# Latent and dilated attention in one pipeline, with norm factors moved into transposes and exponents

## The chip, the cores and the metric

The kernel runs on one core of a Trainium2 chip. A core has TensorE (PE, matrix products and transposes into PSUM), VectorE (DVE), ScalarE (ACT) and GpSimd (Pool), which work from queues of their own and wait for one another by semaphores, and DMA queues, most of them issued by SyncE (SP). The metric is the device time of one execution in microseconds, as the median over several executions. Lower is better.

## The reference, cut to what matters

The program computes two transformer blocks on 256 tokens of 1024 channels. The first block has an even layer, an odd layer and an MLP behind each. The change touches the mixers of these two layers:

```
def even_mixer(h, ...):            # 256 x 1024
    u = h @ w_in                   # 1024 x 2976
    c_q, c_kv, k_r, u_dil = ...    # 384, 256, 32 and 2304 columns
    q = rms_norm(c_q, q_lat_norm) @ w_uq        # 8 heads x (64 + 32)
    kv = rms_norm(c_kv, kv_lat_norm) @ w_ukv    # 8 heads x (64 + 64)
    k = concatenate([k_nope, broadcast(k_r)])   # one k_r for all heads
    q, k = rms_norm(q, mla_qn), rms_norm(k, mla_kn)
    q, k = rope on the last 32 of 96 columns of each
    o_a = dense_causal_attention(q, k, v_a)     # scale 96 ** -0.5
    qd = apply_rope(rms_norm(qkv[:, :, 0], dil_qn), positions)
    kd = apply_rope(rms_norm(qkv[:, :, 1], dil_kn), positions)
    o_b = dilated_mixture(qd, kd, v_d)          # 3 groups x 4 heads of 64
    return concatenate([o_a, o_b]) @ w_out      # 768 x 1024
```

The dilated mixture is a softmax over the keys of three groups together. The odd mixer has 4 differential heads (two softmaxes each) and 8 block heads, all with 64 channels and, at 256 tokens, plain causal masks.

## The kernel before

Tokens lie in two tiles of 128 partitions. A product with weights is made of three products of halves (`mm3`, lines 346 to 348): a weight block arrives by DMA (`raw`), ACT rounds it (`whi`, line 268), DVE subtracts (`wlo`, line 270), and PE multiplies. Weight blocks stand in one sequence through the program; between them stand the *items* of the modulation: half of a 1 MB block of `in_ada_w`, which DVE multiplies and sums in one instruction (lines 308 and 324). They are needed much later, and `spread` sets them among the weight blocks. Of the even stage's 24 items the last 16 are held back to stand ahead of the out projection (`late`), and `tick(n)` takes up n of them.

A recording layer notes every operation of a stage and then sets an order for each engine by priorities and dependences; each engine runs its own queue strictly in that order. So the order can be listed, but not an engine's times.

The even stage (`even`, from line 972) runs: projections 0 to 2 of `w_in` (`dil(i)` for the later ones), whose columns go to `ulat` (latents and `k_r`) and `ud` (dilated q, k and v); the norms of the latents, their transposes (`lh`, `ll`), the products with `w_uq` and `w_ukv`; `normrope` for q and k. `normrope` squares on ACT, sums on DVE (line 685), takes the reciprocal root on DVE in small steps (lines 385 to 390), multiplies by table A, which holds the norm weights and the cosine (691), adds the part that Pool rotated with table B (688, 692), and multiplies by the reciprocal root (693). The tables are made on Pool (lines 666 to 673) from the cosine and sine that ACT computes. Projections 3 and 4 follow, and then a pipeline over four pairs of latent heads with five steps: transposes of q and k (`m_qk`), scores (`m_s`, line 351 through `causal_scores`), maxima, exponents and scaling by the inverse sum (`m_e`), transposes of P (`m_t`), products with v (`m_o`). `pipe` runs step s of job j at turn j + s. Projection 5 and the dilated `normrope` (`dprep`) stand between its first turns. A second pipeline of the same form over four dilated heads follows it (`d_qk` to `d_o`), and behind it the out projection (`out_mm`) and the residual.

A causal mask is added in PSUM by a product with the identity (`masks`, bf16, 128 rows), ahead of the product of q and k (float32, which takes two PE instructions a block). Score tiles come from a pool of two, small PSUM tiles `pt` and `pg` from pools of two each. `cp` puts three of four copies on ACT and the fourth on DVE.

## Time and profile before

| | us |
|---|---|
| median of 3 runs (2333.54 to 2338.28) | 2334.09 |
| the profiled execution | 2334.84 |
| its span, first to last instruction | 2333.0 |
| PE busy in the span | 2210.0 (95%) |
| DVE busy | 1922.9 (82%) |
| ACT busy | 1378.4 (59%) |
| Pool busy | 201.6 (9%) |
| mean granted clock of PE | 0.971 |

The rows that the text rests on are in a section of their own below. In a timeline a row begins with its start and its duration in microseconds, both counted from the start of the span; rows of the same kind in sequence are joined (x4). The duration of one instruction reaches beyond the start of the next where they overlap. The even stage ends near 246 us, the odd stage runs from about 440 to 600.

### The profile page before, as it was taken

The page shows a single profiled execution, that of the slowest core. Times are in us where ns is not written, and L with a number is a line of the kernel's source. Part 1 is how long each engine was busy: PE and PEld are TensorE (multiplying, and loading weights), DVE is VectorE, ACT ScalarE, POOL GpSimd, SP SyncE. Part 2 cuts the span into 40 slices and gives each one's busy share as a digit, 9 for nine tenths or more (in the row PEclk, how much of TensorE's full clock was granted, in tenths as well). Part 3 has the DMA queues.
Part 4 walks back from the last instruction along what each step waited for, and adds up shares of the span by engine and source line. Part 5 has one row for each costly group of instructions (what it writes and reads, how often), then busy time and mean ns, then how long its engine had stood idle before and what let it go on. Part 6 is the DMA issues. An engine that isn't in the chain of part 4 may idle for free. (4 is left out here: it accounts for less than half of the span.)

```text
span 2333.0 us, 30681 instructions
## 1 busy us (share of the span) xinstructions
PE 2210.0 (95%) x11405; PEld 1821.6 (78%) x11405; DVE 1922.9 (82%) x2616; ACT 1378.4 (59%) x1884; POOL 201.6 (9%) x276
## 2 busy tenths in 40 slices
PE   4979999999999997999999999999999999999997
PEld 3766888777788896579997788888878878788875
DVE  6984889687798667669866799999888899898996
ACT  4532644555645534444444678787777776777764
POOL 1320001311200121110000100000000000000010
PEclk9986999999999999999999999999999999999998
DMA  8641798661679398249936799999989989898981
GB/s 330 227 166 64 267 349 320 206 237 51 228 290 355 144 307 235 67 179 376 373 140 261 281 358 371 338 378 340 361 320 368 356 337 365 327 363 339 363 313 55
DMA packets 102333, 647.44 MB, mean 278 GB/s; under 512 B 12037, under 2 KB 19685, under 8 KB 28064
## 3 DMA queue, kind: packets, MB, share of 16 engines
q1 hardware_dynamic: 88512, 618.83, 70.0%
q0 software_dynamic: 12976, 25.41, 4.4%
q8 instruction: 91, 1.49, 0.2%
q10 hardware_dynamic: 688, 1.16, 0.2%
q14 instruction: 66, 0.54, 0.1%
HBM read 637.21 MB, written 8.15 MB: 277 GB/s over the span
## 5 line engine op out<-in xcount | busy, mean ns | idle before, releaser
L270 DVE TENSOR_TENSOR wlo<-raw,whi 128x1024 fp32r<-128x1024 f32 (+1 forms) x551 | 662.5, 1228 | 125.8 <-ACT whi L268 117.8
L268 ACT CAST whi<-raw 128x1024 fp32r<-128x1024 f32 (+1 forms) x551 | 561.8, 1049 | 339.8 <-PE pg L347 94.3
L270 DVE TENSOR_TENSOR wlo<-rawm,whi 128x1024 fp32r<-128x1024 f32 x422 | 505.9, 1238 | 37.0 <-ACT whi L268 25.4
L268 ACT CAST whi<-rawm 128x1024 fp32r<-128x1024 f32 x422 | 426.3, 1052 | 82.7 <-PE sc L348 30.6
L346 PE MATMUL pg<-th,whi 128*128 128x256 f32 x1024 | 293.8, 291 | 2.5 <-ACT th L527 1.8
L347 PE MATMUL pg<-tl,whi 128*128 128x256 f32 x1024 | 293.3, 287 | 0.6 <-DVE tl L522 0.6
L348 PE MATMUL pg<-th,wlo 128*128 128x256 f32 x1024 | 292.9, 287 | 0.4 <-DVE wlo L270 0.4
L346 PEld LDWEIGHTS pg<-th,whi 128*128 128x128 f32 x1024 | 198.3, 195 | 9.7 <-issue 3.3
L347 PEld LDWEIGHTS pg<-tl,whi 128*128 128x128 f32 x1024 | 200.2, 196 | 4.9 <-issue 2.0
L348 PEld LDWEIGHTS pg<-th,wlo 128*128 128x128 f32 x1024 | 200.1, 195 | 1.4 <-DVE wlo L270 1.2
L347 PE MATMUL sc<-wlo,xo 128*128 128x512 f32 x448 | 179.2, 400 | 8.4 <-DVE wlo L270 8.4
L347 PE MATMUL sc<-wlo,th 128*128 128x512 f32 x448 | 177.0, 395 | 2.8 <-DVE wlo L270 2.8
L348 PE MATMUL pg<-whi,gg 128*128 128x512 f32 x448 | 175.9, 393 | 3.5 <-PEq L2095 3.5
L347 PE MATMUL pg<-wlo,gg 128*128 128x512 f32 x448 | 178.8, 399 | 0.0
L346 PE MATMUL sc<-whi,xo 128*128 128x512 f32 x448 | 176.8, 395 | 0.0
L346 PE MATMUL sc<-whi,th 128*128 128x512 f32 x448 | 176.4, 394 | 0.0
L348 PE MATMUL sc<-whi,xo 128*128 128x512 f32 x448 | 175.8, 392 | 0.0
L348 PE MATMUL sc<-whi,th 128*128 128x512 f32 x448 | 175.0, 391 | 0.7 <-POOL th L1991 0.7
L346 PE MATMUL pg<-whi,gg 128*128 128x512 f32 x448 | 161.1, 392 | 1.4 <-ACT gg L369 1.4
L347 PE MATMUL po<-wlo,ah 128*128 128x512 f32 x344 | 134.3, 391 | 1.1 <-DVE wlo L270 1.1
L346 PE MATMUL po<-whi,ah 128*128 128x512 f32 x344 | 135.2, 393 | 0.0
L348 PE MATMUL po<-whi,al 128*128 128x512 f32 x344 | 133.9, 389 | 0.0
(549 smaller groups left out, 3938.1 us busy)
## 6 DMA issues: line engine op xcount, KB each, us to landing
rawm<-in_moe_w SPq DMA_DIRECT2D x196, 1024.0 KB, 6.4
raw<-in_moe_w SPq DMA_DIRECT2D x140, 1024.0 KB, 6.4
raw<-in_mlp_w SPq DMA_DIRECT2D x64, 1024.0 KB, 7.0
raw<-in_ada_w SPq DMA_DIRECT2D x48, 1024.0 KB, 8.4
raw<-in_w_ada SPq DMA_DIRECT2D x35, 1024.0 KB, 6.8
raw<-in_ffn_w SPq DMA_DIRECT2D x20, 1024.0 KB, 8.0
rawm<-in_w_ada SPq DMA_DIRECT2D x13, 1024.0 KB, 6.6
rawm<-in_ffn_w SPq DMA_DIRECT2D x13, 1024.0 KB, 8.2
```

The source lines that it names most:

```text
L268: self.order(self.nc.scalar.copy(h, src))
L270: self.order((self.nc.gpsimd if pool else self.nc.vector).tensor_sub(l, src, h.bitcast(F32)))
L346: mm(out, a[0], b[0], start=start, stop=False, skip_group_check=True)
L347: mm(out, a[0], b[1], start=False, stop=False, skip_group_check=True)
L348: return mm(out, a[1], b[0], start=False, stop=stop, skip_group_check=True)
```

## The change

In the even stage:

- `k_r` is rotated once, for all heads (`kr`), with the rotated part from Pool (`kt`). The sum of squares of k is that of its 64 own columns (`ksq`, squared on ACT) plus that of `k_r` (`kss`).
- The weights of the norms on the first 64 columns of q and k become one column factor `gc`, with which ACT scales k's transposes as it copies them out of PSUM. Table A is applied to q's last 32 columns only.
- q's reciprocal root is no longer multiplied into q; it goes into the maxima and into the scale of the exponent (`qr`, `factors`). One chain of small steps gives the roots of q and k together.
- Copies of v, of ud and of q's and k's transposes are on ACT.
- One pipeline runs over eight jobs, first the four latent pairs, then the four dilated heads, with projection 5 and `dprep` between its turns and the out projection of the latent heads at turns 9 and 10. Value products of some jobs are written into the free quarter of a score tile (`put`). 24 items are held back in place of 16, and six turns take up four each.

In both stages `causal_scores` treats the two heads of a job block by block, both masks first, and the value products of two heads alternate.

```diff
+    def turned(self, src, nh, d, rd, tabs, rt):
+        Bt, n, o = tabs[1], rd // 2, d - rd
+        for h in range(2):
+            b = Bt[:, :, None, h * n:(h + 1) * n].to_broadcast([128, 2, nh, n])
+            self.nc.gpsimd.tensor_tensor(rt[:, :, :, h * n:(h + 1) * n], src[:, :, :, o + (1 - h) * n:o + (2 - h) * n],
+                                         b, ALU.mult)
...
-        for u, (q, k) in enumerate(units):
-            r = ps[:, u]
-            self.mm(r[:, 0:128], self.eyeb, self.cmask(0), True, False)
-            self.mm(r[:, 0:128], q[:, 0:128], k[:, 0:128], False, True)
-            self.mm(r[:, 128:256], q[:, 128:256], k[:, 0:128], True, True)
-            self.mm(r[:, 256:384], self.eyeb, self.cmask(0), True, False)
-            self.mm(r[:, 256:384], q[:, 128:256], k[:, 128:256], False, True)
+        for c, a, b in ((0, 0, 0), (128, 1, 0), (256, 1, 1)):
+            if a == b:
+                for u in range(2):
+                    self.mm(ps[:, u, c:c + 128], self.eyeb, self.cmask(0), True, False)
+            for u, (q, k) in enumerate(units):
+                self.mm(ps[:, u, c:c + 128], q[:, a * 128:a * 128 + 128], k[:, b * 128:b * 128 + 128], a != b, True)
...
-        nc.vector.tensor_scalar(mx, mx, -scale, None, op0=ALU.mult)
+        if factors:
+            m = mx.rearrange("p (a b) -> p a b", a=2)
+            nc.vector.tensor_tensor(m, m, factors[1], ALU.mult)
+            sc = [[factors[0][:, t, u:u + 1] for t in range(2)] for u in range(2)]
+        else:
+            nc.vector.tensor_scalar(mx, mx, -scale, None, op0=ALU.mult)
+            sc = 2 * [2 * [scale]]
...
-            nc.scalar.activation(P[:, u, 0:128], ps[:, u, 0:128], AF.Exp, bias=mx[:, u:u + 1], scale=scale,
+            nc.scalar.activation(P[:, u, 0:128], ps[:, u, 0:128], AF.Exp, bias=mx[:, u:u + 1], scale=sc[u][0],
                                  accum_out=sm[:, u:u + 1])
-            nc.scalar.activation(P[:, u, 128:384], ps[:, u, 128:384], AF.Exp, bias=mx[:, 2 + u:3 + u], scale=scale,
...
-                        n.cp(ud[:, t, c0 + k - 672:c0 + w - 672], ps[:, k:])
+                        nc.scalar.copy(ud[:, t, c0 + k - 672:c0 + w - 672], ps[:, k:])
...
+            kr = lat.tile([128, 2, 32], F32, name="kr")
+            kt = lat.tile([128, 2, 32], F32, name="kt")
+            kss = lat.tile([128, 2, 1], F32, name="kss")
+            own = ulat[:, :, 640:672]
+            nc.scalar.activation(kt, own, AF.Square)
+            nc.vector.reduce_sum(kss, kt, axis=AX.X)
+            n.turned(own[:, :, None], 1, 32, 32, (None, tk[1]), kt[:, :, None])
+            nc.vector.tensor_tensor(kr, own, tk[0][:, :, 64:], ALU.mult)
+            nc.vector.tensor_tensor(kr, kr, kt, ALU.add)
+            gc = ph.tile([96, 2], F32, name="gc")
+            nc.gpsimd.memset(gc, 1.0)
+            for i, nm in enumerate(("mla_q_norm", "mla_k_norm")):
+                nc.gpsimd.dma_start(gc[0:64, i:i + 1], dram(n.I[nm], 0, [[1, 64], [1, 1]]))
+            nc.gpsimd.tensor_tensor(gc[:, 0:1], gc[:, 0:1], gc[:, 1:2], ALU.mult)
...
+                nc.scalar.activation(ksq[:, t], pv[:, :, :64], AF.Square)
                 nc.scalar.copy(k[:, t, :, :64], pv[:, :, :64])
-                nc.vector.tensor_copy(v[:, t], pv[:, :, 64:])
-                nc.gpsimd.tensor_copy(k[:, t, :, 64:], ulat[:, t, None, 640:672].to_broadcast([128, 8, 32]))
+                nc.gpsimd.tensor_copy(k[:, t, :, 64:], kr[:, t, None].to_broadcast([128, 8, 32]))
+                nc.scalar.copy(v[:, t], pv[:, :, 64:])
-            for src, tab, w in ((q4, tq, tmp), (k, tk, ulat)):
-                n.normrope(src, 8, 96, 32, tab, w[:, :, :768].rearrange("p t (h c) -> p t h c", c=96),
-                           w[:, :, 768:].rearrange("p t (h c) -> p t h c", c=32))
+            ss = ph.tile([128, 2, 16], F32, name="qss")
+            sq = tmp[:, :, :768].rearrange("p t (h c) -> p t h c", c=96)
+            rt = tmp[:, :, 768:].rearrange("p t (h c) -> p t h c", c=32)
+            nc.scalar.activation(sq, q4, AF.Square)
+            nc.vector.reduce_sum(ss[:, :, 0:8], sq, axis=AX.X)
+            n.turned(q4, 8, 96, 32, tq, rt)
+            nc.vector.reduce_sum(ss[:, :, 8:], ksq, axis=AX.X)
+            nc.vector.tensor_tensor(ss[:, :, 8:], ss[:, :, 8:], kss.to_broadcast([128, 2, 8]), ALU.add)
+            n.rstd(ss, ss, 96)
+            nc.vector.tensor_tensor(k, k, ss[:, :, 8:, None].to_broadcast([128, 2, 8, 96]), ALU.mult)
+            nc.vector.tensor_tensor(q4[:, :, :, 64:], q4[:, :, :, 64:], tq[0][:, :, None, 64:].to_broadcast([128, 2, 8, 32]), ALU.mult)
+            nc.vector.tensor_tensor(q4[:, :, :, 64:], q4[:, :, :, 64:], rt, ALU.add)
+            ph.tile([128, 56], F32, name="even_out")
+            qr = ph.tile([128, 2, 2, 8], F32, name="qr")
+            for i, f in enumerate((96 ** -0.5, -96 ** -0.5)):
+                nc.vector.tensor_scalar(qr[:, i], ss[:, :, 0:8], f, None, op0=ALU.mult)
...
+                d = att.tile([128, 6, T], F32, name="qk", bufs=2)
+                for i, src in enumerate((q4, k)):
...
+                    nc.scalar.activation(d[:96, 2 * i:2 * i + 2], p[:96], AF.Copy, scale=gc[:, 0:1] if i else 1.0)
+                return d[:, 0:2], d[:, 2:4]
...
-                return n.causal_exp(st, 96 ** -0.5, att)[0]
+                return n.causal_exp(st, None, att, factors=[qr[:, i, :, 2 * j:2 * j + 2] for i in range(2)])[0]
...
+            def put(j):
+                return room[j + 3][:, 3] if j + 3 in room else n.ps.tile([128, 512], F32, name="pg", tag="g")[:, :T]
...
-            next(main)
-            dprep(qd, tdq)
-            dil(5)
-            oT += [n.big.tile([128, KB, T], F32R, name=nm, tag=nm) for nm in ("th", "tl")]
-            next(main)
-            next(main)
-            dprep(kd, tdk)
-            for _ in main:
-                n.tick(2)
+                po = put(j)
+                for i in range(2):
+                    for u in range(2):
+                        n.mm(po[64 * u:64 * u + 64, 128 * i:T], v[:, i, 2 * j + u], st[u][:, T * i:T + 128 * i], i == 0, i == 1)
+                if not oM:
+                    oM.append(n.big.tile([128, 2, 4, T], F32R, name="oM", tag="xn"))
+                n.split(oM[0][:, 0, j], oM[0][:, 1, j], po)
...
+                d = att.tile([128, 6, T], F32, name="qk", bufs=2)
+                for i in range(3):
+                    p = n.ps.tile([128, 2, T], F32, name="pt", tag="t")
+                    for a in range(2):
+                        src, g = ((qd, kd)[(2 * i + a) // 3], (2 * i + a) % 3)
                         for t in range(2):
-                            n.tp(p[:, 0, t * 128:(t + 1) * 128],
+                            n.tp(p[:, a, t * 128:(t + 1) * 128],
+                    n.cp(d[:, 2 * i:2 * i + 2], p)
+                dT[j // 2] = d[:, 0:3], d[:, 3:6]
+                return dT[j // 2]
...
+                p1 = room[4 + j] = n.pa.tile([128, 4, T], F32, name="sc", tag="acc")
...
+                n.order(nc.vector.reduce_max(mx[:, 0:1], p0[:, :384], axis=AX.X))
...
+                r = put(4 + j)[b:b + 64]
                 for g in range(3):
-                    n.mm(r[:, :T], vd[:, 0, g * 4 + j], st[g][:, 0:T], g == 0, False)
+                    n.mm(r, vd[:, 0, g * 4 + j], st[g][:, 0:T], g == 0, False)
                     n.mm(r[:, 128:T], vd[:, 1, g * 4 + j], st[g][:, T:384], False, g == 2)
-                if u:
...
-            for _ in n.pipe(4, [d_qk, d_s, d_e, d_t, d_o]):
-                n.tick(2)
-            acc = n.out_acc()
-            n.out_mm(acc, ("eout", 0), oT, range(0, 4), 0, True, False)
-            n.out_mm(acc, ("eout", 1), oT, range(4, 6), 0, False, True, (0, 2))
+            def both(m, d):
+                return lambda j, st: m(j, st) if j < 4 else d(j - 4, st)
+            acc = []
+            for i, _ in enumerate(n.pipe(8, [both(*f) for f in ((m_qk, d_qk), (m_s, d_s), (m_e, d_e), (m_t, d_t), (m_o, d_o))])):
+                if i == 0:
+                    dprep(qd, tdq)
+                elif i == 1:
+                    dprep(kd, tdk)
+                elif i == 3:
+                    dil(5)
+                    oT += [n.big.tile([128, KB, T], F32R, name=nm, tag=nm) for nm in ("th", "tl")]
+                elif i == 9:
+                    acc = n.out_acc()
+                    n.out_mm(acc, ("eout", 0), (oM[0][:, 0], oM[0][:, 1]), range(0, 2), 0, True, False)
+                elif i == 10:
+                    n.out_mm(acc, ("eout", 0), (oM[0][:, 0], oM[0][:, 1]), range(2, 4), 2, False, False)
+                if 3 <= i < 9:
+                    n.tick(4)
+            n.out_mm(acc, ("eout", 1), oT, range(0, 2), 0, False, True, (0, 2))
...
-                for m in range(2):
-                    h = 2 * (j - 4) + m
-                    r = po[64 * m:64 * m + 64]
-                    n.mm(r[:, :T], vm[:, 0, h], st[m][:, 0:T], True, False)
-                    n.mm(r[:, 128:T], vm[:, 1, h], st[m][:, T:384], False, True)
+                for i in range(2):
+                    for m in range(2):
+                        n.mm(po[64 * m:64 * m + 64, 128 * i:T], vm[:, i, 2 * (j - 4) + m], st[m][:, T * i:T + 128 * i], i == 0, i == 1)
...
-        (b1.even, lambda: b1.even_items(), side(0), 16, ("eout", 0)),
+        (b1.even, lambda: b1.even_items(), side(0), 24, ("eout", 0)),
```

Three places show the new order. DVE, while the latents are normalised; `lss` is the sum of squares of the latents, `tmp` their scaled copy. Before:

```order
L385 TENSOR_SCALAR rsa<-lss 128x2
L1016 TENSOR_SCALAR tmp<-ulat,lss 128x384
L386 TENSOR_SCALAR lss<-rsa 128x2
L1016 TENSOR_SCALAR tmp<-ulat,lss 128x384
L388 TENSOR_TENSOR rsu<-lss 128x2
```

and now:

```order
L1052 TENSOR_TENSOR kr<-ulat,tkA 128x64
L270 TENSOR_TENSOR wlo<-raw,whi 128x768
L385 TENSOR_SCALAR rsa<-lss 128x2
L1050 TENSOR_REDUCE kss<-kt 128x2
L386 TENSOR_SCALAR lss<-rsa 128x2
L388 TENSOR_TENSOR rsu<-lss 128x2
L1053 TENSOR_TENSOR kr<-kr,kt 128x64
L389 SCALAR_TENSOR_TENSOR rsu<-rsu,rsa 128x2
```

The two operations on `kr`, the second of which reads Pool's `kt`, now stand inside the reciprocal root of the kv latents.

PE, behind the fifth projection (512 columns) and around the last (416 columns), before, where the last projection ends:

```order
L347 MATMUL pg<-wlo,th 128x416
L348 MATMUL pg<-whi,tl 128x416
L355 MATMUL pt<-eye,k 96x128 x4
L355 MATMUL pt<-eye,q 96x128 x4
L355 MATMUL pt<-eye,k 96x128 x4
L351 MATMUL sc<-kT,qT 128x128 x2
```

and now, where the fifth ends:

```order
L347 MATMUL pg<-wlo,th 128x512
L348 MATMUL pg<-whi,tl 128x512
L355 MATMUL pt<-eye,q 96x128 x3
L355 MATMUL pt<-eye,k 96x128 x4
L351 LDWEIGHTS eyeb
L351 MATMUL sc<-masks,eyeb 128x128
```

The transposes of k moved ahead of all but one product of the last projection.

PE, among the dilated scores, before:

```order
L351 LDWEIGHTS eyeb
L351 MATMUL pg<-masks,eyeb 128x128
L351 MATMUL pg<-kT,qT 128x128
L351 LDWEIGHTS eyeb
L351 MATMUL sc<-masks,eyeb 128x128
L351 MATMUL sc<-kT,qT 128x128
```

and now, where they begin:

```order
L355 MATMUL pt<-eye,P 128x128 x6
L351 MATMUL pg<-PT,v 64x256 x2
L351 MATMUL pg<-PT,v 64x128 x2
L351 LDWEIGHTS eyeb
L351 MATMUL pg<-masks,eyeb 128x128
L351 MATMUL pg<-qk 128x128
```

The dilated scores now follow a latent pair's transposes of P and value products, and the next pair's follow them.

## Rows read from the trace of the kernel before

**Rows 1.** Busy time by stretch: stretch, length, each engine, granted clock (PEclk), DMA.

```profile
83.50:115.24 31.74, 29.73 (x130) 23.22 (x129) 31.74 (x45) 18.81 (x21) 2.72 (x2) 1.00 0.63 221
115.24:135.96 20.72, 15.88 (x82) 14.72 (x81) 19.18 (x23) 4.04 (x7) 8.78 (x4) 0.84 0.56 201
135.96:170.00 34.04, 25.03 (x148) 19.45 (x147) 31.86 (x83) 18.02 (x54) 4.04 (x8) 0.85 0.35 115
170.00:212.00 42.00, 40.61 (x137) 26.33 (x136) 15.14 (x33) 12.06 (x27) 0.00 (x0) 0.51 0.23 84
212.00:240.60 28.60, 27.15 (x130) 19.65 (x129) 17.06 (x22) 7.79 (x14) 2.27 (x2) 1.00 0.43 166
260.00:280.00 20.00, 20.00 (x151) 19.24 (x151) 19.69 (x21) 13.79 (x19) 0.00 (x0) 1.00 0.99 378
520.00:560.00 40.00, 40.00 (x235) 31.05 (x234) 30.74 (x80) 22.10 (x74) 2.55 (x2) 1.00 0.20 69
```

**Rows 2.** Timeline of DVE: start, us, engine, line, operation, [idle before <-releaser].

```profile
94.77 1.28 DVE L1049 COPY v<-py 128x512 f32<-128x512 f32 x2
...
99.69 1.75 DVE L691 TENSOR_TENSOR k<-k,tkA 128x1536 f32<-128x1536 f32 x1
...
104.57 1.28 DVE L324 SCALAR_TENSOR_TENSOR acc<-raw,cs,acc 128x1024 f32<-128x1024 f32 x1
...
105.85 1.22 DVE L270 TENSOR_TENSOR wlo<-raw,whi 128x1024 fp32r<-128x1024 f32 x1
...
127.25 1.75 DVE L693 TENSOR_TENSOR k<-k,hss 128x1536 f32<-128x1536 f32 x1
...
135.96 0.42 DVE L716 TENSOR_REDUCE mx<-sc 128x2 f32<-128x256 f32 x1 [1.45 <-PE sc L351]
```

**Rows 3.** Timeline of PE around the last projection.

```profile
115.24 0.60 PE L355 MATMUL pt<-eye,q 128*96 128x128 f32 x4
115.59 0.44 PE L346 MATMUL pg<-whi,th 128*128 128x416 f32 x1
...
129.06 1.06 PE L355 MATMUL pt<-eye,k 128*96 128x128 f32 x4 [4.17 <-DVE k L693]
```

**Rows 4.** Timeline of PE, dilated scores.

```profile
172.17 0.29 PE L351 MATMUL pg<-masks,eyeb 128*128 128x128 bf16 x1
...
173.11 0.29 PE L351 MATMUL sc<-masks,eyeb 128*128 128x128 bf16 x1
```

**Rows 5.** Timeline of PE: scores in the even stage, then in the odd stage.

```profile
144.38 0.22 PE L351 MATMUL sc<-masks,eyeb 128*128 128x128 bf16 x1 [3.30 <-ACT P L724]
144.43 0.66 PE L351 MATMUL sc<-kT,qT 96*128 96x128 f32 x4
...
546.39 0.71 PE L351 MATMUL sc<-kT,qT 64*128 64x128 f32 x4
547.03 0.23 PE L351 MATMUL sc<-masks,eyeb 128*128 128x128 bf16 x1
547.19 0.48 PE L351 MATMUL sc<-kT,qT 64*128 64x128 f32 x2
547.61 0.23 PE L351 MATMUL sc<-masks,eyeb 128*128 128x128 bf16 x1
```

**Rows 6.** Timelines of Pool (the rope tables) and DVE (the kv latents).

```profile
65.72 0.96 POOL L669 TENSOR_TENSOR tqA<-gq,cos 128x16 f32<-128x16 f32 x1 [0.43 <-ACT cos L409]
...
79.49 0.29 POOL L673 TENSOR_SCALAR tdkB<-tdkB 128x32 f32<-128x32 f32 x1
...
72.59 0.71 DVE L1017 TENSOR_SCALAR tmp<-ulat,lss 128x256 f32<-128x256 f32 x2
```

**Rows 7.** Timeline of PE behind the out projection.

```profile
240.58 0.60 PE L355 MATMUL pt<-eye,x 128*128 128x128 f32 x4
```

**Rows 8.** Groups by line from 100 to 241 us, ACT: count | busy, mean ns | idle.

```profile
L361 ACT COPY qT<-pt 96x512 f32<-96x512 f32 x4 | 2.3, 582 | 9.0 <-PE pt L355 9.0
...
L722 ACT ACTIVATE P<-sc,mx 128x128 f32<-128x128 f32 x8 | 2.9, 368 | 1.1 <-DVE mx L718 1.1
```

More of the change, by code (lines that the diff above doesn't have):

```diff
@@ L721, in causal_exp @@
         for u in range(2):
-            nc.scalar.activation(P[:, u, 0:128], ps[:, u, 0:128], AF.Exp, bias=mx[:, u:u + 1], scale=scale,
+            nc.scalar.activation(P[:, u, 0:128], ps[:, u, 0:128], AF.Exp, bias=mx[:, u:u + 1], scale=sc[u][0],
                                  accum_out=sm[:, u:u + 1])
-            nc.scalar.activation(P[:, u, 128:384], ps[:, u, 128:384], AF.Exp, bias=mx[:, 2 + u:3 + u], scale=scale,
+            nc.scalar.activation(P[:, u, 128:384], ps[:, u, 128:384], AF.Exp, bias=mx[:, 2 + u:3 + u], scale=sc[u][1],
                                  accum_out=sm[:, 2 + u:3 + u])
@@ L759, in start @@
         self.sm = e(self.tc.tile_pool(name="sm", bufs=4, reuse_waits="tile"))
-        self.sm.tile([128, 48], F32, name="even_out", bufs=1)
+        self.sm.tile([128, 16], F32, name="even_out", bufs=1)
         self.big = e(self.tc.tile_pool(name="big", bufs=1, reuse_waits="tile"))
@@ L1132, in d_s @@
                 p0 = n.ps.tile([128, 512], F32, name="pg", tag="g")
-                p1 = n.pa.tile([128, 4, T], F32, name="sc", tag="acc")
+                p1 = room[4 + j] = n.pa.tile([128, 4, T], F32, name="sc", tag="acc")
                 for g in range(3):
```

38 lines of the change are left out of this document (6 added, 32 removed).

## The prediction

> **What bounds the kernel now.** I read the busy time by stretch first, because the page's shares average over stages with different limits. TensorE (PE) is busy 40.00 of 40.00 us in the odd stage's attention and 20.00 of 20.00 just after the even stage [rows 1]; so what the even stage gives back is not taken up by a wait behind it, and the whole gain is read from two places. In the even stage three stretches are not like that. From 83.50 to 115.24 VectorE (DVE) is busy every microsecond and PE 29.73 of 31.74; from 115.24 to 135.96 PE has 15.88 of 20.72; from 135.96 to 170 PE has 25.03 of 34.04. Then, from 170 to 212, PE is 97% busy but with a granted clock of 0.51, the lower of its two levels (1.2 of 2.4 GHz) [rows 1].
>
> The timelines say why. DVE's queue carries the whole normalisation of q and k between the splits of weights: k's last factor runs only at 127.25 [rows 2]. PE has finished the last projection that needs nothing of it: its products end at 124.89, and the k transposes at 129.06 waited 4.17 us for that factor [rows 3]. The first maximum of the first pair of heads comes at 135.96 [rows 2]. The four latent pairs then pass a short pipeline (PE waits), the clock falls, and the dilated scores run at the low level without a wait to speak of. In them one mask and its product take 0.94 us (172.17 to 173.11) [rows 4]; in the odd stage, at clock 1.00, a mask (0.16) and the first two passes behind it (0.42) take 0.58 [rows 5].
>
> **The change, part by part.** The sum has three terms.
>
> *Until the first maximum.* Ahead of k's last factor DVE loses: the multiply of all of k by its table (1.75, about 1.67 from start to start), the last factor on q (of the same size), two thirds of q's table multiply (1.1), k's rope addition (0.6), the copies of v (1.2), a third of k's reduction (0.5) [rows 2]; five items of the modulation (1.28 each [rows 2], 1.2 with the overlap of the next, so 6.0), which are now held back until the attention; and one or two copies of ud (0.6), now on ScalarE (ACT). That is some 13.5 us. The new small ones (two on kr, a sum, two on qr, wider reciprocal roots) give back about 1. k's factor then ends near 116 in place of 129, just when PE finishes the fifth projection: PE starts the q transposes at 115.24 [rows 3]. The order now puts k's transposes right there and the last projection behind the first scores. From k's transposes to the first maximum it was 6.9 us (129.06 to 135.96) at a falling clock [rows 2, 3], with an evacuation of 0.6 among it; at full clock, and with each pair's scores in one run, about 3.5. So the first maximum comes at 115.24 + 0.35 + 3.5 = 119: 17 us sooner, while the last projection's 9.3 us of PE (115.59 to 124.89) move behind it.
>
> The change also adds a wait. DVE's second operation on kr needs Pool's rotated part, which stands behind all rope tables in Pool's queue; behind it in DVE's queue stand the reciprocal root and the scaling of the kv latents (at 72.59 before), and PE waits for these. Pool started the tables when the cosine came (65.72) and ended at 79.8 [rows 6]; 1.7 us of this were rope work on k that is gone. If the cosine came no sooner, DVE would wait until 78.5, 5.9 us. But two splits (1.22 each), one modulation item and a copy no longer stand ahead of the cosine's last step (some 3.9 us) [rows 2], and the bias DMA, which waits for a buffer in SyncE's queue, no longer stands ahead of the next weights. So Pool ends between 70 and 74.6, against a DVE that gets there at 69 to 72: the cost is 0 to 5. The same shorter queues take away some of PE's small waits before 115 (2 of its 31.74 us there [rows 1]). I set the two against each other and keep 115.24.
>
> *From the first maximum to the end of the out projection.* It took 240.58 − 135.96 = 104.6 us [rows 2, 7]. PE's work in it, turned to full clock by the granted one: 25.03 × 0.85 = 21.3, 40.61 × 0.51 = 20.7, 27.15 at 1.00 [rows 1], and the last projection's 9.3: 78.5 us. One pipeline over eight jobs gives PE other pairs to work on while one pair's maximum, exponent and scaling run; two thirds of the out projection now lie among the last pairs. How full PE will be is the choice that weighs most. It was 0.74 in the stretch from 135.96 and 1.00 in the odd stage, which has the same form: eight jobs, five steps, 77% of DVE beside it [rows 1]. Here DVE has 64.1 us in the old stretch, plus eight more items (9.6), less the evacuations that go to ACT (some 4): 70 of 87, or 80%. I take 0.90, nearer the odd stage, since form and DVE's load are its own: 78.5 / 0.90 = 87.2, so the end is at 119 + 87.2 = 206.2, 34.4 sooner than 240.6 (this contains the 17). The ends: 1.00 gives 43, 0.80 gives 23.
>
> ACT gets k's evacuations with a scale, squares of 512 columns and copies of v and ud, some ten operations of 0.58 [rows 8], about 6 us, in a stretch where it was busy 18.81 of 31.74 [rows 1]; PE's work covers it, and where the cover fails it costs at most these 6. The exponents take their factor from a tile now; one of 128 columns took 0.37 us with the bias alone so [rows 8], sixteen of them beside PE work, so I cost the new operand at nothing. The Trainium skill (ScalarE: Activation LUTs, What ACT_TABLE_LOAD costs) says that each such operand adds about 93 ns; its formula for one operand, 0.39 us, agrees with the row. By it the sixteen exponents would add an estimated 1.5 us to ACT, and the sum would be at most 1.5 higher.
>
> *The odd stage.* Its scores go through the same function. Behind a mask the first two passes of a product take 0.42, the next two 0.22 (0.64 for four), and the mask itself 0.16 to the next start [rows 5]; with 96 rows in the even stage a mask takes 0.05 [rows 5]. A run of masks thus costs about 0.20 + 0.10 = 0.30. Both heads' masks together make two runs of four: 0.60 in each of 8 jobs, 4.8 us of a PE that is full. Ends: 2, if the second head's products keep the longer start, and 10, if heads on different rows or columns run partly side by side.
>
> Sum: 34.4 + 4.8 = 39.2 against the profiled execution's 2334.84 (span 2333.0, 1.8 around it; the median of the runs is 0.75 lower): 2295.6. I predict **2296**.
>
> **The rivals.**
>
> *The low clock stays in the dilated scores.* For it: they took 38 us at the low level with PE full, so a full PE alone does not raise it. Against: in the odd stage heads of 64 rows run at 1.00, and the last projection, 9.3 us of dense products, now stands right ahead. Price: 36 pairs of mask and product × (0.94 − 0.58) = 13, with the transposes and value products of these pairs up to 21; I take 16: 2312.
>
> *DVE's queue becomes the bound.* Four modulation items (4.8 us) in each of six steps stand between a pair's maximum and its scaling. If PE waits for half of them: 6 × 2.4 = 14: 2310. For it: 80% of DVE. Against: the odd stage's 77% with PE full.
>
> *More in the odd stage.* What it would be if the two heads' products, now next to each other on different rows, ran side by side: twelve passes of 0.11 in each job, half of them saved, 0.65 × 8 = 5.2 more: 2290. No row shows it. The Trainium skill (TensorEngine Tiling (Array Packing), Key Properties) says that a change of tiling mode drains TensorE, which the 0.42 against 0.22 bears out, and that different tiles can execute in parallel, which is this rival.
>
> *The edit of the scores does nothing:* 2300, if the cost of a run of masks just moves to the next product; it lies in the forecast's range.
>
> *Slower: waits keep the clock low in the whole merged stretch.* Place: from the first maximum on PE takes its turns in a fixed order, and a wait for DVE (a scaling behind four items) stops all pairs; if each step holds one, the clock stays at the low level as from 170 to 212 [rows 1]. Price: 78.5 × 0.94 / 0.58 = 127, / 0.90 = 141: end at 260, 20 later than before, less 4.8: 2350. It decides from a stretch of 127 us on (it was 104.6). Against it: no stretch but 170 to 212 is wholly low.
>
> **How the numbers follow.** Forecast 2284 to 2306, with the edit that does nothing: 0.50, most likely at 2296. More in the odd stage or a PE fuller than 0.95 (2280 to 2290): 0.12. Low clock: 0.19. DVE's queue: 0.11. Small gain or none (both of the last two, and the wait on kr with 5): 0.03, about 2330. Slower: 0.05. The range, 2280 to 2316, leaves out the last two and the tails of the others, 2 in 10 at most. A measurement tells 0.2% (4.7 us) from no change: faster 0.92, same 0.03, slower 0.05.
>
> **What would show it.** Right: the first maximum near 119; k's transposes straight behind the fifth projection; granted clock near 1.00 from 119 to 206 and PE 0.9 busy; residual transposes at 206; 2.1 us for a job's scores in the odd stage in place of 2.74. Wrong: DVE idle at 70 for Pool's kt; PE waits named after scalings with modulation items ahead; a mask and product at 0.94 again. The forecast falls if PE's share in the merged stretch is under 0.8, or if later stages take the gain back.

## The result, and the profile after

| | before | after |
|---|---|---|
| median (lowest to highest of 5 runs each) | 2333.54 (2323.37 to 2338.28) | 2307.22 (2298.07 to 2311.33) |
| the profiled execution | 2334.84 | 2298.07 |
| its span | 2333.0 | 2296.2 |
| mean granted clock of PE | 0.971 | 0.979 |

The ratio is 0.9891, 95% interval 0.9866 to 0.9915: 26 us faster by the medians, where 38 were forecast. The two profiled executions differ by 36.8, but after's was its fastest and before's is among its slower ones. So I place the difference first. The same matmul, found by its place in PE's sequence, starts so much earlier in the changed kernel (us): behind the even stage 26.1, at the start of the odd stage's attention 26.3, at its end 27.2. Up to there the profile agrees with the medians; the other 10 us come later, in code that the change doesn't touch and that differs from run to run. A second profile of the changed kernel (below) has 28.9 in the span.

Busy time by stretch, after (stretch, length, each engine, granted clock, DMA), the answer to [rows 1]:

```profile
83.50:109.55 26.05, 26.05 (x117) 21.22 (x116) 25.32 (x35) 17.38 (x22) 4.70 (x4) 1.00 0.63 224
114.47:140.00 25.53, 23.54 (x160) 20.45 (x158) 25.42 (x50) 13.10 (x37) 7.33 (x9) 1.00 0.47 161
140.00:160.00 20.00, 18.49 (x88) 11.99 (x88) 14.98 (x34) 6.72 (x19) 0.00 (x0) 0.76 0.56 186
160.00:180.00 20.00, 18.88 (x67) 11.37 (x67) 9.83 (x20) 5.05 (x10) 0.00 (x0) 0.59 0.51 191
180.00:214.06 34.06, 30.88 (x141) 21.16 (x140) 24.90 (x40) 14.49 (x26) 1.53 (x2) 0.98 0.56 201
```

The chain that the prediction followed, after: DVE's sum on kr with its wait for Pool; on PE the end of the fifth projection, k's transposes, the end of the out projection; on DVE k's factor and the first maximum:

```profile
69.21 0.23 DVE L1053 TENSOR_TENSOR kr<-kr,kt 128x64 f32<-128x64 f32 x1 [4.23 <-POOL kt L681]
106.15 1.76 DVE L1093 TENSOR_TENSOR k<-k,qss 128x1536 f32<-128x1536 f32 x1
114.47 0.41 DVE L725 TENSOR_REDUCE mx<-sc 128x2 f32<-128x256 f32 x1
```

```profile
109.55 0.49 PE L355 MATMUL pt<-eye,q 128*96 128x128 f32 x3
109.87 0.60 PE L355 MATMUL pt<-eye,k 128*96 128x128 f32 x4
...
214.06 0.60 PE L355 MATMUL pt<-eye,x 128*128 128x128 f32 x4
```

Up to the first maximum it went better than forecast. From 83.5 to the end of the fifth projection PE is busy every microsecond (26.05 of 26.05; before 29.73 of 31.74 to the same place [rows 1]). k's factor is ready at 107.91, 2.0 us before k's transposes on PE begin (109.87); before, PE waited 4.17 us for it [rows 3]. The first maximum comes at 114.47 (before 135.96 [rows 2]). From there to the residual's transposes it is 99.6 us (before 104.6 [rows 2, 7]), and in that stretch the clock is at 0.76 and 0.59 for 40 us.

The odd stage on PE, one job, the answer to the second half of [rows 5], and two stretches at the start of its attention:

```profile
533.73 0.28 PE L351 MATMUL sc<-masks,eyeb 128*128 128x128 bf16 x2
533.94 0.72 PE L351 MATMUL sc<-kT,qT 64*128 64x128 f32 x8
534.59 0.28 PE L351 MATMUL sc<-masks,eyeb 128*128 128x128 bf16 x2
534.80 0.49 PE L351 MATMUL sc<-kT,qT 64*128 64x128 f32 x4
535.23 0.55 PE L355 MATMUL pt<-eye,P 128*128 128x128 f32 x3
```

```profile
505.00:515.00 10.00, 7.60 (x51) 5.50 (x50) 7.66 (x20) 3.02 (x12) 0.00 (x0) 0.86 0.30 106
515.00:525.00 10.00, 9.83 (x60) 7.43 (x60) 5.84 (x20) 5.37 (x22) 0.00 (x0) 0.63 0.00 0
```

A job's scores took 1.50 us (533.73 to 535.23) in place of 2.74. Eight passes over the rows of two heads took 0.65 (533.94 to 534.59), as four of one head took before (546.39 to 547.03 [rows 5]): the two heads ran side by side. Over eight jobs that is 9.9 us. And yet the odd stage's attention, from its first transposes to those of the residual, took 82.9 us (483.91 to 566.83) against 83.9 before (510.19 to 594.09), only 1.0 less: PE, full in this stage before, now waits and has a lower clock for a while.

### The profile page after: what moved, and what is told of

Read it like the earlier page. It is cut to its first block, busy times and chain, and to the rows that moved or that the text cites. A ratio compares the mean times of both kernels' runs of the same rounds, so it can differ in the third digit from the quotient of the medians.

```text
span 2296.2 us, 30679 instructions
## 1 busy us (share of the span) xinstructions
PE 2186.0 (95%) x11405; PEld 1802.1 (78%) x11405; DVE 1918.0 (84%) x2602; ACT 1382.8 (60%) x1890; POOL 198.9 (9%) x280
```

## The experiments

The first theory was that the score edit and the merged even stage each gain by themselves, and that the shortfall is the low clock in the dilated scores. Its rivals: that ACT's or DVE's queue is the next bound there, that the odd stage gives its gain back whatever is done, and, of the 26 us, that a single one of the parts brings nearly all.

All kernels were timed beside the kernel before on the same chip. "Even" and "odd" say how much earlier than before the even stage, and the odd stage's attention, ended in the profiled execution (the same matmul's start).

| kernel | median (lowest to highest, runs) | ratio, 95% interval | even | odd |
|---|---|---|---|---|
| score edit alone | 2319.01 (2310.45 to 2328.25, 12) | 0.9961, 0.9942 to 0.998 | 0.4 | 8.8 |
| all but the odd stage's score edit | 2320.89 (2308.26 to 2325.64, 11) | 0.996, 0.9941 to 0.9979 | 24.2 | 7.7 |
| dilated scores over all rows | 2288.93 (2281.58 to 2293.52, 4) | 0.9841, 0.9818 to 0.9864 | 41.9 | 41.6 |
| dilated masks in runs | 2292.85 (2291.81 to 2293.22, 4) | 0.9852, 0.983 to 0.9874 | 30.7 | 32.3 |
| two pipelines | 2318.14 (2306.06 to 2319.26, 5) | 0.9923, 0.9895 to 0.9952 | 15.1 | 14.1 |
| items early | 2320.80 (2315.55 to 2325.83, 10) | 0.9952, 0.9934 to 0.9969 | 8.2 | 7.9 |
| masks in runs, everywhere | 2298.75 (2290.66 to 2302.47, 4) | 0.9863, 0.9833 to 0.9893 | 32.0 | 36.1 |
| the changed kernel again | 2306.45 (2294.32 to 2309.97, 6) | 0.988, 0.985 to 0.9909 | 25.2 | 25.9 |
| padded dilated q | 2296.49 (2289.72 to 2300.17, 6) | 0.9845, 0.9816 to 0.9874 | 36.5 | 37.3 |
| padded q in both stages | 2298.77 (2295.18 to 2302.72, 6) | 0.9859, 0.9832 to 0.9887 | 35.8 | 35.2 |
| items held, alone | 2325.22 (2314.64 to 2330.59, 11) | 0.9968, 0.9948 to 0.9987 | 8.2 | 6.3 |
| a later odd stage | 2347.48 (2339.02 to 2351.08, 9) | 1.0066, 1.0045 to 1.0087 | -0.3 | -12.1 |

The last column and the difference of the medians agree within 3.5 us in each row: behind the odd stage's attention nothing more is gained or lost.

### The score edit alone, and everything else

The kernel before, with the new order of the scores in causal_scores and of the odd stage's value products, and nothing else:

```
-        for u, (q, k) in enumerate(units):
-            r = ps[:, u]
-            self.mm(r[:, 0:128], self.eyeb, self.cmask(0), True, False)
-            self.mm(r[:, 0:128], q[:, 0:128], k[:, 0:128], False, True)
...
+        for c, a, b in ((0, 0, 0), (128, 1, 0), (256, 1, 1)):
+            if a == b:
+                for u in range(2):
+                    self.mm(ps[:, u, c:c + 128], self.eyeb, self.cmask(0), True, False)
+            for u, (q, k) in enumerate(units):
+                self.mm(ps[:, u, c:c + 128], q[:, a * 128:a * 128 + 128], k[:, b * 128:b * 128 + 128], a != b, True)
```

> The kernel before with only the new block order of causal_scores and the alternating value products of the odd stage. A job's scores in the odd stage should take about 1.5 us in place of 2.74, as in the changed kernel. Theory A (in the odd stage another engine's chain, ACT's exponents and copies, is late next, and takes the freed time): 0 to 3 us faster than the kernel before, with new PE waits named after ACT between 500 and 560. Theory B (the prediction's: PE alone is the bound there): 5 to 10 us faster.

And the changed kernel with the old order in the odd stage:

```
-                return n.causal_scores([(st[0][64 * m:64 * m + 64]
+                return n.causal_scores_old([(st[0][64 * m:64 * m + 64]
```

> The changed kernel with the odd stage's scores and value products in the old order; the even stage is as changed. Theory A (the odd stage gave 0 to 3): the same as the changed kernel within 3 us, some 24 to 27 under the kernel before. Theory B (the odd stage gave 5 or more): 5 to 10 us slower than the changed kernel.

Alone, the edit brought 8.8 us, 8.6 of it in the odd stage's attention (75.3 us against 83.9), which kept a clock of 1.00 throughout. So the 9.9 read from one job are real, and the side-by-side passes with them. Without it, the changed kernel's even stage still gained 24.2, but the odd stage took 16.5 of that back: 2.1 ahead of its attention and 14.4 in it (98.3 us against 83.9). Its busy time by stretch in this kernel:

```profile
500.00:520.00 20.00, 19.92 (x97) 15.50 (x97) 16.50 (x32) 6.72 (x17) 2.55 (x2) 0.94 0.31 106
520.00:530.00 10.00, 9.83 (x38) 7.21 (x37) 4.05 (x15) 4.91 (x21) 0.00 (x0) 0.50 0.00 0
530.00:540.00 10.00, 9.80 (x44) 7.86 (x43) 4.50 (x16) 3.67 (x18) 0.00 (x0) 0.59 0.00 1
540.00:550.00 10.00, 10.00 (x43) 7.77 (x43) 4.62 (x14) 4.05 (x18) 0.00 (x0) 0.58 0.01 2
550.00:560.00 10.00, 9.38 (x56) 6.41 (x54) 5.93 (x20) 6.01 (x22) 0.00 (x0) 0.91 0.00 0
```

PE is busy 19.92 of 20 us in the stretch in which the clock falls and 29.63 of the next 30, which are at the low level for the most part; no wait brought it down. The code of these jobs is that of the kernel before, which ran it at 1.00 [rows 1]. So in the changed kernel the odd stage's edit is worth some 16 us (by the ratios, 0.996 against 0.9891, of 2333; by their intervals it could be 7 more or less), more than the 5 to 10 of the second expectation: not because it saves 16 but because without it the stage is at the low level for longer.

### What holds the clock low in the dilated scores

In the changed kernel the dilated heads' scores read 64 rows of q and k. The first variant reads all 128; it leaves out the separation of two heads (their scores are summed), with the same number of passes:

```
-                qT, kT = (x[b:b + 64] for x in st)
+                qT, kT = st
```

> The changed kernel with the dilated scores taken over all 128 rows in place of the head's 64, so each score is the sum of two heads' scores: no change of tiling mode between mask and product, the same number of instructions. If the changes of mode keep the clock low: granted clock 1.00 from 140 to 185, a mask and its product 0.28 us, the out projection ends near 195 and the time falls by 15 to 20 us under the changed kernel. If waits for ACT and DVE lower the clock: a shorter PE time only makes more waits, the clock still has stretches at 0.5 between 140 and 185, and the gain is under 10 us.

The second keeps 64 rows and adds the nine masks of a head by three wide instructions ahead of its products (the mask constants are stored in another order for it):

```
+                n.mm(p0[:, :384], n.eyeb, n.masks.rearrange("p (g x c) -> p g x c", x=2, c=128)[:, :, 1], True, False)
+                for g, w in ((0, 2), (2, 1)):
+                    n.mm(p1[:, g:g + w], n.eyeb, n.masks[:, g * T:(g + w) * T], True, False)
                 for g in range(3):
-                    r = p0[:, g * 128:(g + 1) * 128]
-                    n.mm(r, n.eyeb, n.cmask(2 * g), True, False)
...
```

> The changed kernel with the nine masks of a dilated head added by three wide products (384, 512 and 256 columns), so that two runs of masks stand in a head's scores in place of nine; the result is the same. If the price of a run of masks (0.30 us at full clock, more at the low one) is on the path: 28 runs fewer, 8 us or more faster than the changed kernel, and the clock low for a shorter time. If the scaling behind the modulation items or ACT's exponents set the pace there: under 3 us, with longer PE waits named after them.

First a mask and its two passes in the changed kernel, ahead of the low clock and in it:

```profile
144.39 0.22 PE L351 MATMUL pg<-masks,eyeb 128*128 128x128 bf16 x1
144.54 0.49 PE L351 MATMUL pg<-qk 64*128 64x128 f32 x2
144.96 0.23 PE L351 MATMUL pg<-masks,eyeb 128*128 128x128 bf16 x1
...
158.08 0.29 PE L351 MATMUL sc<-masks,eyeb 128*128 128x128 bf16 x1
158.30 0.79 PE L351 MATMUL sc<-qk 64*128 64x128 f32 x2
159.02 0.29 PE L351 MATMUL sc<-masks,eyeb 128*128 128x128 bf16 x1
```

They take 0.57 and 0.94, close to the 0.58 of [rows 5] and the 0.94 of [rows 4]. With all rows, the same stretch by stretch:

```profile
150.00:160.00 10.00, 7.81 (x49) 6.43 (x49) 9.91 (x22) 4.38 (x11) 0.00 (x0) 0.83 0.77 274
160.00:170.00 10.00, 8.50 (x57) 6.08 (x56) 9.45 (x20) 6.78 (x13) 0.00 (x0) 1.00 0.69 236
170.00:180.00 10.00, 8.31 (x35) 4.39 (x35) 9.50 (x20) 4.87 (x11) 0.00 (x0) 1.00 0.53 197
180.00:200.00 20.00, 19.54 (x93) 15.01 (x92) 12.42 (x15) 6.21 (x10) 3.02 (x3) 1.00 0.64 236
```

and in the second profile of the changed kernel:

```profile
150.00:160.00 10.00, 8.97 (x32) 5.30 (x31) 7.45 (x15) 2.31 (x6) 0.00 (x0) 0.50 0.50 156
160.00:170.00 10.00, 8.94 (x32) 5.33 (x32) 4.32 (x10) 2.96 (x8) 0.00 (x0) 0.57 0.45 160
170.00:180.00 10.00, 10.00 (x36) 5.98 (x36) 5.07 (x11) 2.08 (x4) 0.00 (x0) 0.60 0.57 210
```

From 160 to 200 PE is at 1.00 with all rows although it waits 15 to 17% of the time up to 180, and DVE is nearly full behind it; the residual's transposes start at 198.42 in place of 214.06. With 64 rows PE is fuller and at the low level. So it is the scores of 64 rows that take the clock down in this place, not the waits. Is it the 64 rows, or the turn from a mask on 128 rows to a product on 64? The masks in runs have far fewer such turns. They gained too (transposes at 209.60), by fewer instructions, but the clock was as low, which speaks for the rows; some turns are left, so it isn't shown to the end:

```profile
140.00:160.00 20.00, 17.52 (x82) 11.82 (x82) 17.45 (x38) 6.67 (x19) 0.00 (x0) 0.64 0.70 237
160.00:180.00 20.00, 16.81 (x70) 10.86 (x67) 14.13 (x29) 9.57 (x20) 0.00 (x0) 0.68 0.53 184
```

A version that reads 128 rows and computes the same: q of a pair is copied twice, each time with the other head's rows multiplied by zero (k as it is), on top of the masks in runs:

```
+                        nc.scalar.activation(d[:, 2 * i:2 * i + w], p[:, :w], AF.Copy, scale=half[:, 0:1])
+                        nc.vector.tensor_scalar(z[:, 2 * i:2 * i + w], p[:, :w], half[:, 1:2], None, op0=ALU.mult)
...
-                qT, kT = (x[b:b + 64] for x in st)
+                qT, kT = st[j % 2], st[2]
```

> e4_masks_in_runs, and the queries of the dilated heads are copied out of PSUM once for each head, with the other head's 64 rows set to zero by a factor, so that the dilated scores run over 128 rows and stay right: no change of tiling mode in them, for some 1.1 us more of copies a pair. If the products of 64 rows hold the clock low: stretches at 0.5 between 150 and 200 are gone or single, as in e3_full_rows; the out projection ends near 203 to 206, and the total is 6 to 12 us under e4_masks_in_runs. If the larger copies or the waits behind ACT take it back: within 3 us of e4_masks_in_runs.

```profile
150.00:160.00 10.00, 7.23 (x39) 5.79 (x37) 10.00 (x20) 3.69 (x9) 0.00 (x0) 0.68 0.75 266
160.00:170.00 10.00, 8.40 (x54) 5.59 (x52) 8.65 (x19) 5.26 (x11) 2.62 (x5) 0.98 0.70 227
170.00:180.00 10.00, 6.53 (x28) 4.05 (x28) 8.97 (x20) 6.60 (x13) 1.14 (x3) 0.83 0.75 240
180.00:200.00 20.00, 20.00 (x93) 14.63 (x92) 14.19 (x17) 7.37 (x13) 0.00 (x0) 1.00 0.72 273
```

The clock is mostly back here as well, with the heads separated; the transposes start at 203.71. From the first maximum to them, one line each for the changed kernel, the masks in runs, all rows and the padded q:

```profile
114.47:214.06 99.59, 91.78 (x451) 64.98 (x450) 75.13 (x142) 39.36 (x92) 8.86 (x11) 0.86 0.53 186
114.99:209.60 94.61, 84.50 (x427) 61.99 (x426) 75.02 (x142) 39.17 (x92) 8.85 (x11) 0.84 0.56 195
114.56:198.42 83.86, 73.04 (x451) 57.85 (x450) 74.65 (x142) 39.41 (x92) 8.85 (x11) 0.98 0.62 220
115.67:203.71 88.04, 74.52 (x427) 57.55 (x425) 76.14 (x144) 40.97 (x96) 8.87 (x11) 0.94 0.60 210
```

The two kernels whose dilated scores read 64 rows have a clock of 0.86 and 0.84, the two that read 128 rows 0.98 and 0.94, although PE is idle longer in these (10.8 and 13.5 us against 7.8 and 10.1).

With the padded q PE has only 6.5 to 8.4 of 10 us between 150 and 180, and DVE 8.7 to 10.0. DVE's queue may be the next limit of this stretch once the clock is up, but that isn't shown: most of PE's waits there are named after ACT's exponents. In the median the kernel is no better than the masks in runs alone. The same copies in the odd stage:

```
+                            if m:
+                                nc.vector.tensor_scalar(d, p[:, :T], half[:, 1:2], None, op0=ALU.mult)
+                            else:
+                                nc.scalar.activation(d, p[:, :T], AF.Copy, scale=half[:, 0:1])
...
+                return n.causal_scores([(st[m], st[2]) for m in range(2)], ph)
```

> e9_padded_q, and the odd stage's queries are padded in the same way. There heads on the two halves of the rows run side by side now (a job's scores 1.50 us); over 128 rows they can't, and 12 passes of 0.11 with two runs of masks give 1.5 us again. If the products of 64 rows lower the clock in the odd stage too: no stretch at 0.5 between 500 and 545, 3 to 6 us under e9_padded_q. If the wait for ACT there lowers it: the stretch stays, and the eight extra copies cost 0 to 3 us.

No gain over the one before (2298.77 and 2296.49, intervals on each other), though the odd attention kept 1.00 from 500 to 545: the clock of the first expectation with the time of the second. The attention took 80.8 us, against 79.3 at a clock of 0.96 without the copies in this stage. The likely reason, not tested by itself: the two heads' passes on 128 rows follow one another at 0.11 each (in the changed kernel eight took 0.65, with the turn behind the mask), and that costs what the clock gives.

### Which part of the even stage brings the gain

Two pipelines of four jobs one after the other, out projection behind, all else as changed; then the changed kernel with 16 items held back in place of 24:

```
-            for i, _ in enumerate(n.pipe(8, [both(*f) for f in ((m_qk, d_qk), (m_s, d_s), (m_e, d_e), (m_t, d_t), (m_o, d_o))])):
...
+            for _ in main:
+                n.tick(2)
+            for _ in n.pipe(4, [d_qk, d_s, d_e, d_t, d_o]):
+                n.tick(2)
```

> The changed kernel with the two pipelines one after the other, as before (projection 5 and dprep between the first turns, the out projection behind all, items taken up two a turn); norms, factors, copies and score order stay as changed. If the earlier first maximum is what gives (the norms): 15 to 20 us of the even stage's 26.5 stay, the out projection ends near 224. If the merged pipeline is what gives: the out projection ends near 230 to 236, with the dilated scores at 0.5 throughout, as before; the total is 10 to 15 us slower than the changed kernel.

```
-                    n.tick(4)
+                    n.tick(3)
...
-        (b1.even, lambda: b1.even_items(), side(0), 24, ("eout", 0)),
+        (b1.even, lambda: b1.even_items(), side(0), 16, ("eout", 0)),
```

> The changed kernel with 16 items held back, taken up three a turn, so that 8 items go back among the projections, as before. If DVE's queue with four items a turn sets the pace of the merged pipeline (the rival): fewer PE waits behind scalings, out projection some 5 us sooner from the first maximum on, first maximum 5 to 10 us later. If the low clock sets it: stretches at 0.5 between 140 and 185 as in the changed kernel, and the total within 5 us of it or slower by the later first maximum.

And the kernel before with 24 held back, and nothing else:

```
-        (b1.even, lambda: b1.even_items(), side(0), 16, ("eout", 0)),
+        (b1.even, lambda: b1.even_items(), side(0), 24, ("eout", 0)),
```

> The kernel before with one number changed: 24 items of the modulation are held back to the even stage's attention in place of 16; all else as before. In the changed kernel, undoing this cost 14 us and left 8 of the even stage's 26. Theory A, holding back is the largest single part and works alone, since DVE's queue ahead of the first maximum is full: eight items of 1.2 us leave it, k's last factor comes some 10 us before 127.25, the first maximum near 126, the even stage ends 8 to 12 us sooner and the median falls by as much (2320 to 2325). Theory B, it works only together with the normalisation that the change takes off DVE: PE's fifth projection still ends at 113 to 115, q and k wait for their own chain on DVE, the items only move from a stretch where DVE is full to another where it is nearly full (31.86 of 34.04 us from 135.96 to 170), and the median stays within 4 us of the kernel before.

Beside the changed kernel on the same chip (2306.45) two pipelines lose 12 us and early items 14. The first maximum, of two pipelines and of early items:

```profile
125.55 0.41 DVE L725 TENSOR_REDUCE mx<-sc 128x2 f32<-128x256 f32 x1
```

```profile
125.97 0.41 DVE L725 TENSOR_REDUCE mx<-sc 128x2 f32<-128x256 f32 x1
```

Both are 11 us later than 114.5, for different reasons. With two pipelines the last projection stands ahead of the first scores again, 9 us of PE; behind the maximum it is 101 us (transposes at 226.54) without these 9 us of work. There PE is idle 11.9 us in place of 7.8, and its clock is 0.75 in place of 0.86: the merged pipeline saves waits and, by more, time at the low level. The result has something of both expectations: 15.1 us of the even stage's gain stay, as in the first, and the whole is 12 slower, as in the second. With early items k's first transposes come only at 119.51, 9.6 later, because PE and k's factor are both late:

```profile
75.00:90.00 15.00, 11.03 (x49) 9.93 (x48) 13.85 (x30) 7.56 (x12) 3.23 (x7) 0.77 0.62 223
```

PE has 11.03 of 15 us, part of them at the low level, where the changed kernel has 15.00 at 1.00. Holding the items back is therefore worth most ahead of the attention, where PE waits for work that stands behind them on DVE. Alone in the kernel before it moved the first maximum from 135.96 to 129.27 and brought 7.8 us:

```profile
129.27 0.42 DVE L716 TENSOR_REDUCE mx<-sc 128x2 f32<-128x256 f32 x1 [0.68 <-PE sc L351]
```

That lies between the two expectations, nearer the first: it needs nothing else of the change, but k's factor (it starts at 121.31) is still 4 us late for PE.

### Masks in runs in all scores, the changed kernel again, and a later odd stage

The masks in runs, with in causal_scores one product for both masks of a head:

```
+            self.mm(ps[:, u].rearrange("p (x c) -> p x c", c=256)[:, :, :128], self.eyeb,
+                    self.cmask(0)[:, None].to_broadcast([128, 2, 128]), True, False)
```

> e4_masks_in_runs, and in causal_scores one product adds both masks of a head, so that one run of masks stands in a job's scores in place of two; the result is the same. If runs of masks between products of 64 rows keep the clock low and cost 0.30 us each: 8 runs fewer in the odd stage, 2 to 5 us faster than e4_masks_in_runs, and no stretch at 0.5 in the odd attention. If the waits there lower the clock: as e4_masks_in_runs within 2 us.

It gives no more than the masks in the even stage alone (2298.75 and 2292.85 on different chips). The changed kernel a second time, to see which features of its profile return:

> The changed kernel as it is, beside the other three. If the 9 us between its first profile and its median are a matter of which clock windows fall low in a run: a median of 0.989 to 0.991 of the kernel before, a profile whose low stretches lie elsewhere in the even and odd attention, and work in between that takes the same time. If the chip made the difference: another ratio.

They do: first maximum at 114.69, transposes at 214.75, low clock from 150 to 180 (rows above), and the odd attention's start with PE at 7.45 of 10 us and a clock of 0.67:

```profile
510.00:520.00 10.00, 7.45 (x43) 5.25 (x41) 5.63 (x20) 5.91 (x25) 0.00 (x0) 0.67 0.10 40
```

Last, the kernel before with two passes of DVE over part of the odd stage's input, which only delay it:

```
         hT = n.normT(n.x, n.modA(1, 0, n.col["nmix"][:, 8:16]), row=ROW.get(2))
+        for _ in range(2):
+            nc.vector.tensor_scalar(hT[1], hT[1].bitcast(F32), 1.0, None, op0=ALU.mult)
```

> The kernel before with DVE passing over the low halves of the odd stage's input twice ahead of its projections, a delay of about 4.4 us and nothing else. e2_even_alone lost 16 us in the odd stage's old code although PE waited for nothing there. If that is a matter of when the stage starts: the odd attention of this kernel has stretches at 0.5 that the kernel before didn't show, and it is slower than before by 8 us or more. If the changed even stage does it in another way: 4 to 5 us slower, no stretch at 0.5 between 510 and 560.

The attention began 11.2 us later (521.35) and ended 12.1 later, in place of the 4.4 meant, since the clock also fell while PE waited (0.77 from 465 to 480). It then kept 1.00 (40.00 busy of 40.00 from 520 to 560) and took 84.8, against 83.9. So a later start doesn't by itself bring the low clock of the changed kernel's odd stage. Nor does an earlier one of some us: the kernel before with the items held begins the attention 6.4 us earlier, and runs it as before:

```profile
503.84:587.80 83.96, 83.16 (x448) 64.43 (x447) 64.41 (x150) 43.69 (x117) 11.14 (x12) 1.00 0.33 120
```

The changed kernel with early items begins it 9.1 us earlier (501.09), little sooner than that, and has a clock of 0.90 in it. What does bring it is open: the 64-row scores lose the clock there after a changed even stage, and not in the kernel before, with the items held or with the score edit alone. In what way the changed even stage does it was not found.

## Why the prediction was right, and where it was too high

*Until the first maximum: right, and by its mechanism; 4.5 us better.* Forecast 119, measured 114.47. DVE's queue was the bound, k's factor met the end of the fifth projection, and k's transposes followed it. I had kept PE's end of the fifth projection at 115.24; it came at 109.55. Of these 5.7 us, 3.4 are PE's small waits from 40 us on (4.3 before, 0.9 now), which the shorter queue on DVE took away: with the items held back and nothing else they are 0.1, and in the changed kernel with early items 5.6. The other 2.3 are the same matmuls in less busy time; why is open. I had netted the small waits against the wait on kr. That wait was there on DVE (4.23, forecast 0 to 5), but behind it PE waited 0.72 in all, so it hardly counted. From k's transposes to the first maximum it took 4.6 us, where I had 3.5.

*From the first maximum to the out projection: the share and the work were right, the clock was wrong.* PE was busy 23.54 + 18.49 + 18.88 + 30.88 = 91.8 of 99.6 us, 0.92 where I took 0.90. Turned to full clock, 23.54 + 18.49 × 0.76 + 18.88 × 0.59 + 30.88 × 0.98 = 79.0, where I had 78.5. The step that failed is the one that turned PE's work to full clock and took that for the time the work would need: the low level added 12.8 us to PE's busy time, and without them the stretch would have ended near 201. This is the rival *the low clock stays in the dilated scores* (price 13 to 21), which I put at 0.19. The argument against it was the odd stage's heads of 64 rows at 1.00. The variant with all rows shows the rival's reason, 15.6 us at the same place; and in the changed kernel, with the odd stage's old score order, that stage's clock fell too, with PE busy 9.8 of 10 us, so its 1.00 was no evidence that scores of 64 rows are safe.

The Trainium skill (TensorE: Matmul & The Clock Gate, HAM oscillation) speaks of idle gaps as what brings the clock down. Here the gaps decided little: with all rows PE was idle 10.8 us from the first maximum on, 2.5 at the longest, and had a clock of 0.98; in the changed kernel it was idle 7.8, 1.5 at the longest, and had 0.86.

*The odd stage: mechanism right, size twice too small, and then lost.* 4.8 was forecast, 9.9 measured by job, since the heads run side by side: the rival *more in the odd stage* (0.12; 4.8 + 5.2) gave 10.0. Alone, 8.8 arrived. In the changed kernel's odd attention only 1.0 did. The rows at the start of the odd attention show one part of the loss:

```profile
511.16 0.71 PE L355 MATMUL pt<-eye,u 128*128 128x128 f32 x4 [2.03 <-ACT qT L361]
512.25 0.37 PE L351 MATMUL sc<-masks,eyeb 128*128 128x128 bf16 x2 [0.38 <-ACT P L739]
```

From 483.91 to 566.83 PE was idle 4.6 us (0.8 before, from 510.19 to 594.09), and by the two stretches from 505 to 525 the low level cost 7.60 × 0.14 + 9.83 × 0.37 = 4.7. The two together, 8.5, are most of what was lost of the 9.9. The Trainium skill (TensorEngine Tiling (Array Packing), Key Properties) says that different tiles can run in parallel; 8 passes in 0.65 us against 4 in 0.64 agree.

*DVE's queue.* The rival that items held back would delay the scalings (0.11) was wrong for this kernel: PE waits 0.7 us for scalings (DVE's `Pd`) from 109 to 215, and held back, the items are worth 14 us of the 26, and 8 alone.

*Sum.* 34.4 + 4.8 was forecast; 26.1 came in the even stage (8 short, which is the 12.8 of the clock less the 4.5 of the first maximum) and about 1 in the odd. 2307.22 lies nearer to the rival's 2312 than to the 2296, and it fell into the range partly by luck: the first maximum came 4.5 us better, which hid a third of the clock's cost. That the odd stage would lose its own gain stood in none of the rivals. The parts are not additive: taking one out of the changed kernel costs 16 (odd scores), 12 (pipeline) or 14 (items), together more than the whole brings.

Two of the experiments' kernels, the masks in runs and the padded dilated q, have ratios of 0.9852 and 0.9845 to the kernel before, against 0.9891 and 0.988 of the changed kernel in its two measurements. Their gains are 35 and 36 us in place of 26, and their intervals just meet those of the changed kernel. On one chip with it only the masks in runs everywhere were timed: 2298.75 against 2306.45.

## What to carry to other kernels

Turn a stretch's work into full-clock time only when you know why its clock was low: if the products that ran at the low level stay as they are, give the low clock the larger chance, however full the engine will be. Work that is not urgent is worth holding back where the bound's feeder has a full queue, even into a stretch that looks nearly full itself. And measure a part both alone and taken out of the whole: here the odd stage's edit brought 9 alone, and next to nothing can be seen of it in the changed kernel's own odd stage, which without it would be 16 slower.

## What the runs showed of the hardware that I had not expected

In the odd stage of the changed kernel without its edit, where scores of 64 rows stand between masks, PE fell to half its clock while it was busy 19.92 of 20 us; in the kernel before the same code ran at 1.00, and what tells the two apart stayed open. In the even stage the same number of passes over 128 rows in place of 64 kept 1.00 from 160 to 180 with PE busy 83 to 85%, where the changed kernel had 0.59. Passes of two heads on different halves of the rows, issued alternately, took no longer than those of one (0.65 for eight, 0.64 for four). And an exponent whose factor comes from a tile took longer, which I had costed at nothing. Groups by line, ACT, after (count | busy, mean ns | idle):

```profile
L739 ACT ACTIVATE P<-sc,mx,qr 128x256 f32<-128x256 f32 x8 | 4.5, 566 | 0.0
L737 ACT ACTIVATE P<-sc,mx,qr 128x128 f32<-128x128 f32 x8 | 3.7, 462 | 1.8 <-DVE mx L729 1.8
```

462 ns against 368 [rows 8], 94 more each; sixteen of them make an estimated 1.5 us of ACT. The Trainium skill's figure of 93 ns for such an operand (ScalarE: Activation LUTs, What ACT_TABLE_LOAD costs) agrees.
